# Split weights kept in device memory: a hybrid GLA/SSD block whose later token blocks load the parts

## The chip, the cores and the metric

The kernel runs on one core of a Trainium2 chip. The metric is device time in microseconds (us) of one execution. A core has five engines that work side by side and wait for each other by semaphores: TensorE (PE, matrix products; its weight loads are shown apart as PEld), VectorE (DVE), ScalarE (ACT), GpSimd (POOL) and SyncE (SP), which here only issues transfers. Transfers from device memory to on-chip memory run on 16 DMA engines.

## The reference

One layer over 2048 tokens of width 1024, in float32. Two mixers share one input projection: a gated linear attention with 4 heads and a state-space scan with 16 heads in two groups. A gated embedding and a last norm follow.

```
u = rmsnorm(h, norm_w)
q, k, v, g, gate_lr, z, xbc, dt_raw = split(u @ w_in)
gla_out = rmsnorm(gla_chunked(q, k, v, log_a)) * silu(g)
xs, bm, cm = split(silu(causal_conv(xbc)))
y = rmsnorm_per_group((ssd_chunked(xs, dt, a_neg, bm, cm) + xs * d_skip) * silu(z))
h = h + concat(gla_out, y) @ w_out
h = h + sigmoid(rmsnorm(h) @ w_pe_gate) * (p @ w_pe)
out = rmsnorm(h)
```

## The kernel before

**Blocks.** The 2048 tokens are cut into NB = 4 blocks of TB = 512, one after the other; the states of both mixers go from block to block. Each block runs through the same 70 pieces of weight, so every weight is read from device memory four times.

**Split products.** A float32 operand is held as two parts of a faster type, `hi` (the value rounded) and `lo` (the rest), and each product is made of three matmuls: hi by hi, hi by lo, lo by hi. In `dense_t` these are L203, L204, L205 (24 matmuls of 512 columns for one weight), in `dense_n` L222, L224, L226 (48 matmuls of 256 or 288 columns), in `out_proj` L794, L795, L796, in the embedding L938, L939, L940. The activations' parts are made once per block; the weights' parts are made anew in each block.

**How a weight comes in.** `plan` (L114) lists the 4 x 70 weights in the order of use. `take_w` (L177) hands out the next one and sees to it that one more is prepared behind it. `prep_w` (L157) allots a raw tile (tag `wraw`, 2 buffers), loads 512 or 576 KB into it from SP's queue (L164), and splits it in two halves: ACT casts the half to `whi` (L172), DVE subtracts to get `wlo` (L173). `whi` and `wlo` have 4 buffers each, so two weights can be held in parts:

```
s = raw[:, i * hn:(i + 1) * hn]
nc.scalar.copy(out=hi, in_=s)
tt(out=lo, in0=s, in1=hi.bitcast(F32), op=ALU.subtract)
```

**Side work.** Recurrences and norms are generators that `step()` (L184) moves on by one piece after each dense product. `ssd_steps` (L510) walks over 4 pieces of 128 tokens: it loads a decay tile `em` twice and `ec` (SP, L550 and L561), turns `em` into the decay mask with four DVE operations (L552), an exponential on ACT (L555) and a product (L556), and TensorE uses it in L579; `em` has 3 buffers. `ec` is used at L588, the state is updated at L587. `gla_steps` (L455) walks over the same pieces for one head: L451 to L453 and L488 on TensorE, L486 on DVE. `u_steps` (L321) loads the next block's input piece by piece (`xp`, SP, L327) and turns it into `u` on DVE (L328), ACT (L329) and POOL (L331). `final_steps` (L608) of a block runs in the next one: DVE writes the result into `ht` (L627) and POOL's queue sends it out in four stores (L629); then SP loads the next block's `ht`, 2 MB, at L851.

**Order.** The program is written in the order above; a scheduler with a time model of its own then sets each engine's order among what the dependences allow, and each engine and each queue runs its list strictly in order. So whatever waits at the head of SP's list holds back all transfers behind it. The results of dense products lie in 4 buffers (`psd`), those of the side work in 4 others (`pss`); TensorE waits when the next of them has not been emptied. The copy of the embedding product to `pp` (L941, ACT) is such an emptying.

Of the kernel before, what the change touches and what calls it, by code (L numbers as in the profile page):

```python
# [6 lines left out]
F32 = mybir.dt.float32  # L7
F32R = mybir.dt.float32r
# [3 lines left out]
ALU = mybir.AluOpType  # L12
# [23 lines left out]
def hybrid_kernel(ctx, tc, x_nat, x_t, p_t, w_t, w_n0, w_n, w_o, w_g, w_p, prm, gup, cst, out):  # L36
    nc = tc.nc
    mm = nc.tensor.matmul
    act = nc.scalar.activation
    tt = nc.vector.tensor_tensor  # L40
    stt = nc.vector.scalar_tensor_tensor
    NB = x_t.shape[0]
# [4 lines left out]
    wp = ctx.enter_context(tc.tile_pool(name="wp", bufs=2))  # L47
    sb = ctx.enter_context(tc.tile_pool(name="sb", bufs=2))
# [3 lines left out]
    dr = ctx.enter_context(tc.tile_pool(name="dr", bufs=2, space=DRAM))  # L52
# [45 lines left out]
    for h in range(GH):  # L98
        t = state.tile([P, 256], F32, name=f"gT{h}")
# [3 lines left out]
    for g in range(2):  # L103
        t = state.tile([P, 512], F32, name=f"sS{g}")
# [3 lines left out]
    for h in range(GH):  # L108
        t = sm.tile([P, NT + 1], F32, name="gD", tag=f"gD{h}", bufs=2)
# [3 lines left out]
    LAST_TAGS = {KT - 4: ("qm", "km", "qm", "km"), KT - 3: ("em", "em", "em", "amh")}  # L113
    plan = []  # L114
    for b in range(NB):
        def natural(src):
            plan.extend((src[i], 1152 if src is w_n0 else 1024, None) for i in range(2))

        def tseq(lst, tags=None):
            plan.extend((s, 1024, tags) for s in lst)  # L120

        def oseq(q):
            plan.extend((w_o[q, i], 1024, None) for i in range(4))

        natural(w_n0)
        if b == 0:
            natural(w_n[0])
        tseq([w_t[T_B], w_t[T_C]] + [w_t[T_XS + i] for i in range(2)])
        if b:
            natural(w_n[0])  # L130
        tseq([w_t[T_XS + i] for i in range(2, 4)])
        tseq([w_t[T_Q], w_t[T_K], w_t[T_Q + 1], w_t[T_K + 1]])
        tseq([w_t[T_Z + i] for i in range(4)])
        natural(w_n[1])
        natural(w_n[2])
        tseq([w_t[T_B + 1], w_t[T_C + 1]])
        oseq(2)
        tseq([w_t[T_XS + 4 + i] for i in range(2)])
        natural(w_n[3])
        tseq([w_t[T_XS + 4 + i] for i in range(2, 4)])  # L140
        natural(w_n[4])
        tseq([w_t[T_Q + 2], w_t[T_K + 2]])
        oseq(0)
        natural(w_n[5])
        natural(w_n[6])
        tseq([w_t[T_Q + 3], w_t[T_K + 3]])
        tseq([w_t[T_Z + 4 + i] for i in range(4)])
        oseq(1)
        oseq(3)
        for i in range(8):  # L150
            if i % 4 == 0:
                tseq([w_p[i // 4]])
            tseq([w_g[i]], LAST_TAGS.get(i) if b == NB - 1 else None)
    ready = []
    cursor = [0]

    def prep_w(raw=None):  # L157
        if cursor[0] == len(plan):
            return
        src, n, tags = plan[cursor[0]]  # L160
        cursor[0] += 1
        if raw is None:
            raw = wp.tile([P, n], F32, name="wraw", tag="wraw", bufs=SB["wraw"])
            nc.sync.dma_start(out=raw, in_=src)  # L164
        res = []
        hn = n // 2
        for i in range(2):
            pool, th, tl = (sb, tags[2 * i], tags[2 * i + 1]) if tags else (wp, "whi", "wlo")
            hi = pool.tile([P, hn], F32R, name="whi", tag=th, bufs=SB[th])
            lo = pool.tile([P, hn], F32R, name="wlo", tag=tl, bufs=SB[tl])  # L170
            s = raw[:, i * hn:(i + 1) * hn]
            nc.scalar.copy(out=hi, in_=s)  # L172
            tt(out=lo, in0=s, in1=hi.bitcast(F32), op=ALU.subtract)  # L173
            res.append((hi, lo))
        ready.append(res)
# [495 lines left out]
    for b in range(NB):  # L671
# [188 lines left out]
        v1, _ = dense_v(1)  # L860
# [18 lines left out]
        v3, _ = dense_v(3)  # L879
# [47 lines left out]
        for d, cs in jobs:  # L927
            n = cs.stop - cs.start
            if d % 4 == 0 and cs.start == 0:
                wpe = take_w()  # L930
                pp = sb.tile([P, 4, TB], F32, name="pp", tag="xs", bufs=SB["xs"])
                for j in range(4):
                    pps = psd.tile([P, TB], F32, name="psd")
                    for k in range(2):
                        sl = slice(j * P, (j + 1) * P)
                        hi, lo = wpe[k]
# [11 lines left out]
            th = sb.tile([P, n], F32, name="gth", tag="tmp", bufs=SB["tmp"])  # L948
# [101 lines left out]
```

## Time and profile before

| | before |
|---|---|
| median of 3 runs | 1922.84 us (1921.1 to 1924.56) |
| profiled execution, span | 1915.8 us |
| TensorE busy | 1848.5 us, 96% |
| TensorE's weight loads | 1577.9 us, 82% |
| VectorE busy | 1402.0 us, 73% |
| ScalarE busy | 929.5 us, 49% |
| GpSimd busy | 372.3 us, 19% |
| DMA | 206.56 MB, 108 GB/s over the span |

The span is the profiled execution's own time from its first to its last instruction; the runs are timed from outside, and their median is 7.0 us longer. Busy time is what an engine's instructions cover; matmuls overlap, so a busy TensorE can still be short of its best.

### The profile page before, as it was taken

The numbers are of one execution on the slowest core, as the hardware profiler recorded it, in microseconds if no ns is written. First come the engines' busy times: TensorE is split into PE (matmuls) and PEld (weight loads), VectorE is DVE, ScalarE is ACT, GpSimd is POOL, SyncE is SP. The second block draws the span as 40 slices with busy tenths as digits, with TensorE's granted clock in tenths as the row PEclk, the third lists the DMA queues.
The fourth block names the chain that finished last, engine by engine and source line by source line (L and its number), as shares of the span: only waits on it lengthen the run. The fifth ranks groups of instructions, "written<-read, shape, count | busy, mean of one in ns | idle before, by whom it ended". The sixth has DMA issues, their size and how long they took to land.

```text
span 1915.8 us, 27885 instructions
## 1 busy us (share of the span) xinstructions
PE 1848.5 (96%) x10418; PEld 1577.9 (82%) x10418; DVE 1402.0 (73%) x2689; ACT 929.5 (49%) x1692; POOL 372.3 (19%) x331
## 2 busy tenths in 40 slices
PE   8989999999999999999999999999999999999997
PEld 7868888877887888877788788897778788889886
DVE  8996686587788668558678766855877877684676
ACT  6545443465554553346555355334655445533563
POOL 3022031043112103004311210300430211030122
PEclk9999999999999999999999999999999999999998
DMA  4332242233443233223344323322334432232232
GB/s 138 121 110 88 79 158 73 88 110 122 170 125 100 82 107 125 77 78 110 124 177 121 101 77 115 117 89 77 123 113 165 135 97 78 92 104 82 68 119 77
DMA packets 80888, 206.56 MB, mean 108 GB/s; under 512 B 8048, under 2 KB 26736, under 8 KB 80368
## 3 DMA queue, kind: packets, MB, share of 16 engines
q1 hardware_dynamic: 78768, 198.21, 32.5%
q0 software_dynamic: 1984, 6.55, 0.9%
q8 instruction: 82, 1.34, 0.3%
q14 instruction: 54, 0.44, 0.1%
HBM read 196.09 MB, written 8.65 MB: 107 GB/s over the span
## 4 chain that ended last, share of the span: by engine, by line
PE 70%; DVE 18%; ACT 5%; issue 3%; DMA 3%; POOL 1%; SPq 0%; DVEq 0%; ACTq 0%; POOLq 0%
PE psd L204 10%; PE psd L203 10%; PE psd L205 10%; PE psd L224 5%; PE psd L226 5%; PE psd L222 5%; PE psd L796 5%; PE psd L795 5%; PE psd L794 5%; DVE em L552 3%; DVE wlo L173 3%; PE pss L488 1%; DMA xp<-x_t 1%; DMA em<-cd 1%; DVE em L556 1%
## 5 line engine op out<-in xcount | busy, mean ns | idle before, releaser
L173 DVE TENSOR_TENSOR wlo<-wraw,whi 128x512 fp32r<-128x512 f32 (+1 forms) x560 | 423.9, 761 | 218.7 <-ACT whi L172 217.3
L172 ACT CAST whi<-wraw 128x512 fp32r<-128x512 f32 (+1 forms) x560 | 343.9, 620 | 466.0 <-PE psd L204 238.2
L205 PE MATMUL psd<-u,wlo 128*128 128x512 f32 x896 | 352.7, 394 | 2.1 <-DVE wlo L173 2.1
L203 PE MATMUL psd<-u,whi 128*128 128x512 f32 x896 | 353.7, 395 | 0.0
L204 PE MATMUL psd<-u,whi 128*128 128x512 f32 x896 | 351.8, 393 | 0.9 <-POOL u L331 0.9
L222 PE MATMUL psd<-whi,u 128*128 128x256 f32 (+1 forms) x960 | 276.5, 288 | 0.0
L224 PE MATMUL psd<-wlo,u 128*128 128x256 f32 (+1 forms) x960 | 273.1, 284 | 2.1 <-DVE wlo L173 2.1
L226 PE MATMUL psd<-whi,u 128*128 128x256 f32 (+1 forms) x960 | 272.6, 284 | 0.0
L300 POOL TENSOR_TENSOR sq<-sq,sqt 128x512 f32<-128x512 f32 (+1 forms) x85 | 109.9, 1293 | 610.1 <-ACT sqt L297 610.1
L794 PE MATMUL psd<-mq,whi 128*128 128x512 f32 x512 | 205.4, 402 | 0.0
L796 PE MATMUL psd<-mq,wlo 128*128 128x512 f32 x512 | 202.1, 395 | 0.0
L795 PE MATMUL psd<-mq,whi 128*128 128x512 f32 x512 | 201.0, 393 | 0.0
L205 PEld LDWEIGHTS psd<-u,wlo 128*128 128x128 f32 x896 | 168.5, 188 | 39.4 <-DVE wlo L173 3.9
L204 PEld LDWEIGHTS psd<-u,whi 128*128 128x128 f32 x896 | 168.6, 188 | 34.1 <-POOL u L331 1.2
L203 PEld LDWEIGHTS psd<-u,whi 128*128 128x128 f32 x896 | 168.6, 188 | 33.5 <-ACT whi L172 0.6
L224 PEld LDWEIGHTS psd<-wlo,u 128*128 128x128 f32 x960 | 183.6, 191 | 5.3 <-DVE wlo L173 2.9
L222 PEld LDWEIGHTS psd<-whi,u 128*128 128x128 f32 x960 | 183.6, 191 | 2.4 <-ACT whi L172 1.0
L226 PEld LDWEIGHTS psd<-whi,u 128*128 128x128 f32 x960 | 183.6, 191 | 0.0
L797 DVE TENSOR_TENSOR ht<-ht,psd 128x512 f32<-128x512 f32 x128 | 86.9, 682 | 66.2 <-PE psd L796 65.9
L796 PEld LDWEIGHTS psd<-mq,wlo 128*128 128x128 f32 x512 | 96.3, 188 | 20.6 <-issue 0.7
L203 PE MATMUL psd<-mq,whi 128*128 128x512 f32 (+1 forms) x288 | 107.3, 373 | 5.8 <-ACT pp L941 5.8
L795 PEld LDWEIGHTS psd<-mq,whi 128*128 128x128 f32 x512 | 96.4, 188 | 20.0 <-DVE mq L505 1.1
(248 smaller groups left out, 3274.0 us busy)
## 6 DMA issues: line engine op xcount, KB each, us to landing
wraw<-w_t SPq DMA_DIRECT2D x112, 512.0 KB, 3.5
wraw<-w_o SPq DMA_DIRECT2D x64, 512.0 KB, 3.5
wraw<-w_n SPq DMA_DIRECT2D x56, 512.0 KB, 3.5
em<-cd SPq DMA_DIRECT2D x64, 256.0 KB, 3.9
wraw<-w_g SPq DMA_DIRECT2D x32, 512.0 KB, 3.6
ec<-ecd SPq DMA_DIRECT2D x64, 128.0 KB, 3.0
xn<-x_nat SPq DMA_DIRECT2D x24, 256.0 KB, 3.4
xp<-x_t SPq DMA_DIRECT2D x24, 256.0 KB, 3.8
```

The costliest lines, as they stand in the source:

```text
L172: nc.scalar.copy(out=hi, in_=s)
L173: tt(out=lo, in0=s, in1=hi.bitcast(F32), op=ALU.subtract)
L203: mm(out=ps, lhsT=hi[:, sl], rhs=rhi(k), start=(k == 0), stop=False)
L204: mm(out=ps, lhsT=hi[:, sl], rhs=rlo(k), start=False, stop=False)
L205: mm(out=ps, lhsT=lo[:, sl], rhs=rhi(k), start=False, stop=(k == KT - 1))
L222: mm(out=outs[t], lhsT=ug(0, k)[:, ts], rhs=hi[:, sl], start=first, stop=False, skip_group_check=True)
L224: mm(out=outs[t], lhsT=ug(0, k)[:, ts], rhs=lo[:, sl], start=False, stop=False, skip_group_check=True)
L226: mm(out=outs[t], lhsT=ug(1, k)[:, ts], rhs=hi[:, sl], start=False, stop=last, skip_group_check=True)
L300: self.eng.tensor_tensor(out=self.acc[:, cs], in0=self.acc[:, cs], in1=sq, op=ALU.add)
L794: mm(out=ps, lhsT=hi[:, sl], rhs=mq[:, 0, k, :], start=(k == 0), stop=False)
L795: mm(out=ps, lhsT=hi[:, sl], rhs=mq[:, 1, k, :], start=False, stop=False)
L796: mm(out=ps, lhsT=lo[:, sl], rhs=mq[:, 0, k, :], start=False, stop=(k == 3))
```

## The change

In block 0 (`split_w`) a weight is loaded and split as before, but both parts of a half go into one tile `whl` ([128, 2, n]; 4 buffers, the same bytes as `whi` and `wlo` had), and when the next weight is prepared, `save_w` writes these tiles to device memory from SP's queue: two stores of 512 KB (576 KB for `w_n0`) for each weight. In blocks 1 to 3 (`load_w`) nothing is split: the two halves of parts are loaded, 512 KB each, by two transfers on SP's queue. For two weights of three they go into `whl`, for the third into the buffers of `wraw`, so three weights can be held, and `take_w` prepares two ahead instead of one. The last block's weights with tags of their own come in four transfers of 256 KB. The tile `praw` (L912) moves from the buffers of `wraw` to that of `sg`. Line numbers behind the new functions are greater by 37: L550 is L587, L588 is L625, L627 is L664, L797 is L834, L851 is L888.

```diff
-SB = {"tmp": 4, "wraw": 2, "whi": 4, "wlo": 4, ...
+SB = {"tmp": 4, "wraw": 2, "whl": 4, ...
...
+    def save_w():
+        while unsaved:
+            dst, t = unsaved.pop(0)
+            nc.sync.dma_start(out=dst, in_=t.bitcast(F32))
+
+    def split_w(src, key, n, raw):
+        if raw is None:
+            raw = wp.tile([P, n], F32, name="wraw", tag="wraw", bufs=SB["wraw"])
+            nc.sync.dma_start(out=raw, in_=src)
+        save_w()
+        hn = n // 2
+        kept[key] = dr.tile([2, P, 2, hn], F32, name="wk_" + "_".join(map(str, key)),
+                            tag="wk_" + "_".join(map(str, key)), bufs=1)
+        res = []
+        for i in range(2):
+            t = wp.tile([P, 2, hn], F32R, name="whl", tag="whl", bufs=SB["whl"])
+            s = raw[:, i * hn:(i + 1) * hn]
+            nc.scalar.copy(out=t[:, 0, :], in_=s)
+            tt(out=t[:, 1, :], in0=s, in1=t[:, 0, :].bitcast(F32), op=ALU.subtract)
+            unsaved.append((kept[key][i], t))
+            res.append((t[:, 0, :], t[:, 1, :]))
+        return res
+
+    def load_w(key, n, tags, at):
+        save_w()
+        hn = n // 2
+        res = []
+        for i in range(2):
+            if tags:
...
+                continue
+            tg = "wraw" if at % 3 == 2 else "whl"
+            t = wp.tile([P, 2, hn], F32R, name="wkl", tag=tg, bufs=SB[tg])
+            nc.sync.dma_start(out=t.bitcast(F32), in_=kept[key][i])
+            res.append((t[:, 0, :], t[:, 1, :]))
+        return res
...
+        ready.append(split_w(src, key, n, raw) if pb_ == 0 else load_w(key, n, tags, at))
 
     def take_w():
-        while len(ready) < 2 and cursor[0] < len(plan):
+        while cursor[0] < len(plan) and len(ready) < (2 if plan[cursor[0]][3] == 0 else 3):
             prep_w()
         return ready.pop(0)
...
-        praw = wp.tile([P, 2 * TB], F32, name="praw", tag="wraw", bufs=SB["wraw"])
+        praw = sb.tile([P, 2 * TB], F32, name="praw", tag="sg", bufs=SB["sg"])
```

The engines' lists change in these places. In a row stand the line, the operation, what it writes and reads (with buffer numbers) and the size.

**SP, block 0, first group of `ssd_steps`** (`wraw` is a raw weight, `wk` a place in device memory, `em` and `ec` the decay tiles). Before:

```order
L164 DMA wraw_1003<-w_t 128x1024
L550 DMA em_970<-cd_846 128x512
L550 DMA em_978<-cd_846 128x512
L561 DMA ec_986<-ecd_848 64x4x128 x2
L550 DMA em_1076<-cd_846 128x512
L164 DMA wraw_1115<-w_t 128x1024
L164 DMA wraw_1366<-w_t 128x1024
L550 DMA em_1084<-cd_846 128x512
```

Now:

```order
L171 DMA wraw_1014<-w_t 128x1024
L166 DMA wk_t_21_937<-whl_938 128x1024
L587 DMA em_981<-cd_855 128x512
L587 DMA em_989<-cd_855 128x512
L598 DMA ec_997<-ecd_857 64x4x128 x2
L166 DMA wk_t_21_937<-whl_941 128x1024
L587 DMA em_1088<-cd_855 128x512
L171 DMA wraw_1127<-w_t 128x1024
L587 DMA em_1096<-cd_855 128x512
L166 DMA wk_t_25_1018<-whl_1019 128x1024
L166 DMA wk_t_25_1018<-whl_1022 128x1024
```

Two stores per weight now stand among the loads of the decay tiles.

**SP and DVE, early in block 1** (`ht` is the block's input of 2 MB; `n_1` is the gate's weight of head 0, used after four other weights). SP before:

```order
L164 DMA wraw_4965<-w_t 128x1024
L164 DMA wraw_5013<-w_n 128x1024
L164 DMA wraw_5077<-w_n 128x1024
L851 DMA ht_5311<-x_t 128x4096
L164 DMA wraw_5135<-w_t 128x1024
```

SP now:

```order
L202 DMA wkl_4967<-wk_t_5_650 128x1024
L202 DMA wkl_5009<-wk_n_1_0_284 128x1024
L888 DMA ht_5319<-x_t 128x4096
L202 DMA wkl_5011<-wk_n_1_0_284 128x1024
L202 DMA wkl_5051<-wk_n_1_1_375 128x1024
L202 DMA wkl_5053<-wk_n_1_1_375 128x1024
```

DVE before, the last block's result:

```order
L627 SCALAR_TENSOR_TENSOR ht_84<-ht_84,pr_82,rbc_4751 128x512
L173 TENSOR_TENSOR wlo_4842<-wraw_4839,whi_4841 128x512
L173 TENSOR_TENSOR wlo_4846<-wraw_4839,whi_4845 128x512
L627 SCALAR_TENSOR_TENSOR ht_84<-ht_84,pr_82,rbc_4751 128x512 x2
L173 TENSOR_TENSOR wlo_4918<-wraw_4915,whi_4917 128x512
L627 SCALAR_TENSOR_TENSOR ht_84<-ht_84,pr_82,rbc_4751 128x512
L173 TENSOR_TENSOR wlo_4922<-wraw_4915,whi_4921 128x512
```

DVE now:

```order
L664 SCALAR_TENSOR_TENSOR ht_84<-ht_84,pr_82,rbc_4813 128x512
L846 TENSOR_SCALAR lrn_4750<-psd_4756 128x4x16
L848 SCALAR_TENSOR_TENSOR dtr_4877<-psd_4756,pr_82 128x16
L851 TENSOR_TENSOR v_4872<-psd_4756,v_4872 128x256
L664 SCALAR_TENSOR_TENSOR ht_84<-ht_84,pr_82,rbc_4813 128x512 x7
```

The 2 MB load now stands between the two halves of one weight, and the eight operations that it waits for (by way of the stores) stand together, ahead of the products of the next weights. The same rows come again in blocks 2 and 3.

**DVE, block 1, second group of `ssd_steps`**, where `ec` is multiplied (L588, now L625). Before:

```order
L466 TENSOR_TENSOR amh_7410<-am_7407,amh_7410 128x512
L173 TENSOR_TENSOR wlo_7427<-wraw_7420,whi_7426 128x512
L797 TENSOR_TENSOR ht_5311<-ht_5311,psd_7430 128x512
L797 TENSOR_TENSOR ht_5311<-ht_5311,psd_7444 128x512
L173 TENSOR_TENSOR wlo_7512<-wraw_7509,whi_7511 128x512
L588 TENSOR_TENSOR ec_7398<-ec_7398,pss_7458 128x512
```

Now:

```order
L503 TENSOR_TENSOR amh_7244<-am_7241,amh_7244 128x512
L834 TENSOR_TENSOR ht_5319<-ht_5319,psd_7258 128x512
L834 TENSOR_TENSOR ht_5319<-ht_5319,psd_7272 128x512
L625 TENSOR_TENSOR ec_7232<-ec_7232,pss_7286 128x512
```

The two subtractions ahead of the product are gone, and nothing has come in their place.

## Rows read from the trace of the kernel before

**Rows 1.** The page, parts 1 and 3: busy time by engine; DMA queue, packets, MB, share.

```profile
PE 1848.5 (96%) x10418; PEld 1577.9 (82%) x10418; DVE 1402.0 (73%) x2689; ACT 929.5 (49%) x1692; POOL 372.3 (19%) x331
...
q1 hardware_dynamic: 78768, 198.21, 32.5%
```

**Rows 2.** Waits of TensorE in blocks 1 to 3: us in total, times, longest.

```profile
PE pss L451 <- DVE gT L486: 11.6, 6, 2.0
PE psd L203 <- ACT pp L941: 4.1, 2, 2.4
PE pss L459 <- DVE ec L588: 3.0, 3, 1.0
PE pss L267 <- POOL sq L300: 2.6, 2, 1.3
PE pss L451 <- DVE ec L588: 2.2, 2, 2.0
...
PE psd L224 <- DVE wlo L173: 1.6, 3, 0.5
PE psd L205 <- DVE wlo L173: 1.6, 3, 0.5
...
PE pss L451 <- DVE sS L587: 1.1, 3, 0.4
...
PE psd L940 <- DVE wlo L173: 0.9, 2, 0.6
```

**Rows 3.** Groups by line: busy us, mean ns of one, idle before.

```profile
L173 DVE TENSOR_TENSOR wlo<-wraw,whi 128x512 fp32r<-128x512 f32 (+1 forms) x560 | 423.9, 761 | 218.7 <-ACT whi L172 217.3
```

**Rows 4.** Timeline of block 1 from 768 us, DVE and TensorE: start, duration.

```profile
768.49 1.53 DVE L173 TENSOR_TENSOR wlo<-wraw,whi 128x512 fp32r<-128x512 f32 x1
...
771.14 0.68 DVE L173 TENSOR_TENSOR wlo<-wraw,whi 128x512 fp32r<-128x512 f32 x1
...
772.56 0.36 PE L451 MATMUL pss<-v,amh 128*128 128x256 f32 x1 [2.03 <-DVE ec L588]
```

**Rows 5.** One line's durations (min/median/max ns), then the timeline from 1056 us.

```profile
L552 DVE TENSOR_SCALAR em<-em,cum x256: 264/279/1528, 88.4 to 1713.0; 128x128 f32<-128x128 f32 x128
...
1056.13 3.48 DVE L552 TENSOR_SCALAR em<-em,cum 128x128 f32<-128x128 f32 x4
...
1060.00 0.39 PE L451 MATMUL pss<-v,kn 128*128 128x256 f32 x1 [1.94 <-DVE gT L486]
```

**Rows 6.** Timeline of block 1's end, DVE and TensorE.

```profile
937.34 0.75 DVE L328 SCALAR_TENSOR_TENSOR xp<-xp,pr,urb 128x512 f32<-128x512 f32 x1 [0.56 <-DMA xp<-x_t]
...
939.42 0.50 PE L203 MATMUL psd<-mq,whi 128*128 128x512 f32 x1 [2.36 <-ACT pp L941]
```

**Rows 7.** Stretches: busy us by engine (instructions), TensorE's clock, DMA share, GB/s.

```profile
12.00:485.00 473.00, 456.81 (x2561) 388.00 (x2561) 359.38 (x670) 236.59 (x434) 100.07 (x80) 1.00 0.33 105
...
240.00:288.00 48.00, 46.90 (x310) 40.86 (x308) 38.65 (x73) 21.09 (x44) 14.51 (x16) 1.00 0.47 154
...
768.00:816.00 48.00, 45.97 (x314) 42.12 (x313) 26.38 (x53) 14.85 (x31) 1.60 (x2) 0.96 0.25 77
```

**Rows 8.** Issue to landing of the loads of `em`, and DVE's wait for them.

```profile
  DMA em<-cd: 5.5, 8
...
DMA to landing us min/median/max: 3.0/3.9/6.2
```

**Rows 9.** Timeline of block 1 from 506 us: SP, POOL's queue, TensorE; landing of `ht`.

```profile
512.65 0.53 POOL L629 DMA_DIRECT2D out_t<-ht  x1 [2.18 <-DVE ht L627]
...
516.80 0.33 SPq L851 DMA_DIRECT2D ht<-x_t  x1
...
DMA to landing us min/median/max: 7.8/7.8/7.8
...
521.98 0.28 PE L222 MATMUL psd<-whi,u 128*128 128x256 f32 x1
522.10 0.28 PE L224 MATMUL psd<-wlo,u 128*128 128x256 f32 x1
```

More of the change, by code (lines that the diff above doesn't have):

```diff
@@ L27 @@
 M_ID, M_TRI, M_ONE, M_N = 0, 128, 256, 384
-SB = {"tmp": 4, "wraw": 2, "whi": 4, "wlo": 4, "rb": 1, "urb": 1, "v": 1, "amh": 1, "bc": 2, "sg": 1, "qm": 2, "km": 2, "kn": 1, "st": 2,
+SB = {"tmp": 4, "wraw": 2, "whl": 4, "rb": 1, "urb": 1, "v": 1, "amh": 1, "bc": 2, "sg": 1, "qm": 2, "km": 2, "kn": 1, "st": 2,
       "bt": 1, "ctl": 1, "xs": 1, "cb": 1, "bn": 1, "xd": 2, "xh": 1, "ec": 1, "em": 3, "sq": 1, "lrT": 1}
@@ L116, in natural, with tseq @@
         def natural(src):
-            plan.extend((src[i], 1152 if src is w_n0 else 1024, None) for i in range(2))
-        def tseq(lst, tags=None):
-            plan.extend((s, 1024, tags) for s in lst)
+            if src == 0:
+                plan.extend((w_n0[i], ("n0", i), 1152, b, None) for i in range(2))
+            else:
+                plan.extend((w_n[src - 1, i], ("n", src, i), 1024, b, None) for i in range(2))
+        def tseq(*lst):
+            plan.extend((w_t[j], ("t", j), 1024, b, None) for j in lst)
         def oseq(q):
-            plan.extend((w_o[q, i], 1024, None) for i in range(4))
-        natural(w_n0)
+            plan.extend((w_o[q, i], ("o", q, i), 1024, b, None) for i in range(4))
+        natural(0)
         if b == 0:
-            natural(w_n[0])
-        tseq([w_t[T_B], w_t[T_C]] + [w_t[T_XS + i] for i in range(2)])
+            natural(1)
+        tseq(T_B, T_C, T_XS, T_XS + 1)
         if b:
[L130 to L136, printed above, removed]
-        oseq(2)
[L138 to L142, printed above, removed]
+            natural(1)
+        tseq(T_XS + 2, T_XS + 3)
+        tseq(T_Q, T_K, T_Q + 1, T_K + 1)
+        tseq(*(T_Z + i for i in range(4)))
+        natural(2)
+        natural(3)
+        tseq(T_B + 1, T_C + 1)
+        oseq(2)
+        tseq(T_XS + 4, T_XS + 5)
+        natural(4)
+        tseq(T_XS + 6, T_XS + 7)
+        natural(5)
+        tseq(T_Q + 2, T_K + 2)
         oseq(0)
[L144 to L147, printed above, removed]
+        natural(6)
+        natural(7)
+        tseq(T_Q + 3, T_K + 3)
+        tseq(*(T_Z + 4 + i for i in range(4)))
         oseq(1)
@@ L151, in hybrid_kernel @@
             if i % 4 == 0:
-                tseq([w_p[i // 4]])
-            tseq([w_g[i]], LAST_TAGS.get(i) if b == NB - 1 else None)
+                plan.append((w_p[i // 4], ("p", i // 4), 1024, b, None))
+            plan.append((w_g[i], ("g", i), 1024, b, LAST_TAGS.get(i) if b == NB - 1 else None))
     ready = []
     cursor = [0]
+    kept = {}
+    unsaved = []
+    def save_w():
[25 more added lines that the diff above has]
+            if tags:
+                pair = []
+                for j in range(2):
+                    tg = tags[2 * i + j]
+                    t = sb.tile([P, hn], F32R, name="wsp", tag=tg, bufs=SB[tg])
+                    nc.sync.dma_start(out=t.bitcast(F32), in_=kept[key][i, :, j, :])
+                    pair.append(t)
+                res.append(tuple(pair))
+                continue
[4 more added lines that the diff above has]
+        return res
     def prep_w(raw=None):
@@ L159, in prep_w @@
             return
-        src, n, tags = plan[cursor[0]]
+        src, key, n, pb_, tags = plan[cursor[0]]
+        at = cursor[0]
         cursor[0] += 1
[L162 to L175, printed above, removed]
+        ready.append(split_w(src, key, n, raw) if pb_ == 0 else load_w(key, n, tags, at))
     def take_w():
-        while len(ready) < 2 and cursor[0] < len(plan):
+        while cursor[0] < len(plan) and len(ready) < (2 if plan[cursor[0]][3] == 0 else 3):
             prep_w()
```

## The prediction

> **What bounds the kernel now.** I read the busy times first, then who TensorE waits for, then the timeline around the longest of these waits. TensorE is busy for 1848.5 of 1915.8 us; DVE, which splits the weights, for 1402.0 [rows 1]. So the kernel is bound by TensorE's matmuls, of which the change takes none away, and a lighter DVE is worth only what TensorE waits for it. All that TensorE is idle is 1915.8 - 1848.5 = 67.3 us, its start and end and block 0 among it: more than this can't be had, however much DVE work goes. The list of waits says which part hangs on the splits: in blocks 1 to 3 the waits that bear on this sum to 28.7 us, and only three of the rows (1.6, 1.6 and 0.9 us) name a split itself [rows 2]. The others name an operation that stood in DVE's or ACT's list behind something, and the timeline tells behind what [rows 4 to 6].
>
> **What goes.** 560 subtractions take 761 ns on average [rows 3]; 420 of them, with as many casts on ACT, belong to blocks 1 to 3, some 320 us of DVE time. They lie beside the matmuls, so I cost them by the waits, not by their length.
> 1. The three rows that name a split: 1.6 + 1.6 + 0.9 = **-4.1 us** [rows 2]. The split is gone; what TensorE waits for in its place is a load, which is ordered two weights ahead.
> 2. Waits for `ec` and `sS`, 3.0 + 2.2 + 1.1 = 6.3 us [rows 2]. In block 1 the product for which TensorE waited 2.03 us stood behind splits of 1.53 and 0.68 us [rows 4], and both are missing from DVE's new list there. But the run of DVE work began with the decay tiles, whose part of the delay stays. Bounds 2.2 (that one place) and 6.3; I take **-4.5 us**, nearer to the upper end since in DVE's lists the other places look alike.
> 3. Waits for `gT`, 11.6 us in six [rows 2]. Here DVE was held by four operations on `em`, 3.48 us where the median of one is 279 ns, 1.1 us for four [rows 5]. No split is in that stretch, so most stays. Bounds 0 and 6 x 0.68 = 4.1 (one split of [rows 4] less ahead of each); I take **-2 us**, as one split stands ahead in about half of the cases.
> 4. Waits for `pp` and for the sum of squares, 4.1 + 2.6 = 6.7 us [rows 2]. The copy to `pp` stands in ACT's list behind a cast that waits for `xp`, on whose load DVE was still waiting [rows 6]; the splits that held the SP queue and DVE's list there go, the load's flight stays. Bounds 0 and 6.7; I take **-3 us**, a little under half.
> 5. After the wait of item 2 TensorE ran at half clock (1.2 instead of 2.4 GHz) for a while: 0.96 granted over 48 us [rows 7], so 0.04 x 48 = 1.9 us lost. Bounds 0 and 1.9; if the wait goes, so may this: **-1 us**.
>
> **What comes.**
> 6. Block 0 moves three times the weight bytes. 70 weights are 36.8 MB; the parts are twice that, 73.7 MB, written in 473 us, 156 GB/s more. The queue's 198.21 MB took 32.5% of the span [rows 1], so the engines at full work move 198.21 / (0.325 x 1915.8 us) = 318 GB/s. Block 0 goes from 105 to 261, and its busiest stretch from 154 to 310 GB/s [rows 7], 97% of 318. The Trainium skill (DMA: Bandwidth & Descriptors, Specifications) gives about 358 GB/s as the memory limit of a core; by that figure the stretch would be at 87%, and this item could be near 0. What it costs is the lateness of small loads: `em` lands after 3.9 us as a rule and 6.2 at worst, but DVE waited visibly for it for only 5.5 us in all [rows 8]. Three later pieces in each of two groups, six rounds, each 6.2 - 3.9 = 2.3 us later: 13.8 us if nothing hides it, 0 if all is hidden. I take a third, **+4.6 us**: the tile has a spare buffer, and most landings were hidden so far. The stores themselves wait for a split that SP's next raw load waited for before as well; behind them in SP's list stand raw loads, ordered two weights ahead.
> 7. In blocks 1 to 3 each weight is two loads, 1 MB. That is 105 + 78 = some 183 GB/s, 58% of 318, and a load is issued when the weight three places before it is used up, two weights ahead of need: at 473 us for 70 weights [rows 7] some 13 us, against 3.9 us for a typical landing [rows 8]. So the steady state is covered. The cover is thin at one place: the 2 MB load of `ht` stands before the second half of a weight. It took 7.8 us and was issued at 516.80, after the last store at 512.65; TensorE uses that weight from 521.98 on [rows 9]. In DVE's new list the results are finished in one run, so stores and load should go some 4 us earlier, and the half would land at about 512.6 + 7.8 + 1.6 (512 KB at 318 GB/s) = 522.0, just in time. Bounds 0 and the 10.5 us of the second rival; I take **+1 us**.
> 8. `praw` in another buffer, the wider tile, the four loads of 256 KB at the very end: 0; no row of TensorE's waits names what they touch, and the buffers are free by then.
>
> The sum is -4.1 - 4.5 - 2 - 3 - 1 + 4.6 + 1 = **-9.0 us**: the span goes from 1915.8 to 1906.8, and the median, 7.0 above the profiled span, from 1922.84 to **1913.8 us**, 0.47% less. A measurement of this kernel tells about 0.2%, 3.8 us, from no change.
>
> **The rivals.**
> - *The waits stay.* TensorE's long waits hang on decay tiles and `gT`, not on splits; then only item 1 is gained, block 0 still pays: -4.1 + 4.6 + 1 = +1.5, **1924.3 us**. For it: the largest row names `gT`, with no split in the stretch [rows 2, 5]. Against it: the places of item 2, where the splits can be seen [rows 4].
> - *Slower: the `ht` load blocks half a weight* in each of blocks 1 to 3. If the stores are no earlier than before, `ht` goes at 516.80 and lands 7.8 later, the half behind it 1.6 after that, at 526.2; it is needed six matmuls (0.12 us apart) after 521.98, at 522.7 [rows 9]. Three waits of 3.5 us are 10.5, and three times the half clock of item 5 adds 5.7: +16.2 instead of +1, in all +6.2, **1929.0 us**. It decides if `ht` is issued later than about 513. For it: the list puts it there in all three blocks, and SP can't pass it. Against it: the results come together in DVE's list now. The Trainium skill (DMA: Bandwidth & Descriptors, Queues, rings and completion order) says that a DMA engine takes the descriptors of a ring in order, by which the half could not overtake; that the landing of `em` ranges from 3.0 to 6.2 us on the same queue agrees with it.
> - *Block 0 is saturated.* Item 6 costs its full 13.8: -14.6 + 13.8 + 1 = +0.2, **1923.0 us**; with the first rival's small gain +10.7, **1933.5 us**. For it: 97% in one stretch [rows 7]. Against it: 82% over the block, and `em` was rarely waited for [rows 8].
> - That the splits remain can be ruled out: they are missing from DVE's list.
>
> **How the numbers follow.** The forecast gets 0.58, the first rival 0.14, the second 0.16, the third 0.12, a third of it with the first. Faster by over 0.2% is the forecast: 0.58. Within 0.2% are the first rival and two thirds of the third: 0.22. Slower are the second and the rest of the third: 0.20. The forecast's own range takes the bounds of its items: at best -4.1 - 6.3 - 4.1 - 6.7 - 1.9 with nothing paid, -23.1; all at once is unlikely, and I stop at -20, 1903. At the upper end it meets 1919. The range that holds the time 8 times in 10 reaches on to the second rival: **1903 to 1931 us**.
>
> **What would show it.** Right: 140 subtractions and casts instead of 560; no row of waits for a split after block 0; the waits for `ec` under 3 us in all, those for `gT` still near 10; no half clock at the place of 768 us; SP's queue moving some 382 MB (198 + 184); the idle time of blocks 1 to 3 down by some 14 us and block 0 longer by some 5. Wrong: a new row in which TensorE waits for a load of parts (`wkl`), above all some 33 us into each of blocks 1 to 3; `em` landing after 6 us as a rule in block 0, with DVE waiting; or a block 0 longer by 10 us or more.

## The result: 1902.8 us, faster than forecast

The changed kernel takes **1902.84 us** (median of 4 runs, 1899.13 to 1906.1), the kernel before 1923.38 us beside it: a ratio of 0.9891, 95% interval 0.9872 to 0.991. That is 20.5 us less, where 9.0 were forecast, and just outside the range of 1903 to 1931. The runs below were timed on several chips, each beside the kernel before. To compare them, each ratio to the kernel before is multiplied by 1923.4 us: the change gives **-21.0 us**. The half widths of the intervals are 3 to 5 us, so a difference of two such runs is uncertain by 4 to 6 us.

The page of the changed kernel, parts 1, 3 and 6:

```profile
PE 1840.8 (97%) x10418; PEld 1579.5 (83%) x10418; DVE 1113.7 (59%) x2269; ACT 698.0 (37%) x1272; POOL 355.1 (19%) x331
...
q1 hardware_dynamic: 129744, 382.39, 62.4%
...
wkl<-wk_t SPq DMA_DIRECT2D x168, 512.0 KB, 4.0
...
em<-cd SPq DMA_DIRECT2D x64, 256.0 KB, 4.2
```

DVE is 288.3 us lighter than in [rows 1] and the queue moves the 382 MB that were forecast. TensorE, the engine that bounds the kernel, is busy 7.7 us less with the same 10418 matmuls, and idle 62.0 us in place of 67.3. The splits' row shows 140 in place of the 560 of [rows 3], all in block 0:

```profile
L181 DVE TENSOR_TENSOR whl<-wraw,whl x140: 676/688/1784, 6.6 to 487.5; 128x512 fp32r<-128x512 f32 x136, 128x576 fp32r<-128x576 f32 x4
```

The stretches, in the columns of [rows 7]: block 0, its busiest slice, blocks 1 to 3.

```profile
12.00:485.00 473.00, 449.99 (x2508) 381.83 (x2507) 352.97 (x659) 230.59 (x424) 95.60 (x77) 0.99 0.74 253
240.00:288.00 48.00, 47.51 (x304) 41.83 (x303) 36.20 (x69) 22.52 (x46) 11.03 (x12) 1.00 0.92 307
497.00:1892.00 1395.00, 1372.06 (x7833) 1182.30 (x7831) 743.41 (x1567) 454.31 (x826) 250.59 (x232) 1.00 0.60 188
```

For blocks 1 to 3 the kernel before has this row, which did not stand ahead of the prediction:

```profile
485.00:1904.00 1419.00, 1383.96 (x7834) 1183.38 (x7832) 1030.60 (x1984) 683.73 (x1243) 267.43 (x233) 0.99 0.34 108
```

In the first 473 us TensorE gets through 2508 matmuls in place of 2561: block 0 pays. Afterwards nearly the same 7833 matmuls take 1395 us in place of 1419. TensorE's idle time there falls from 35.0 to 22.9 us, so by 12.1; its *busy* time falls by another 11.9. Block 1 begins with the first product that uses its first weight. From the span's start to there, block 0 is 497.1 us long (485.6 before), and blocks 1 to 3 together are 1405.8 (1430.2): +11.5 and -24.4.

TensorE's waits in blocks 1 to 3 of the changed kernel, from 504 us on, in the columns of [rows 2]:

```profile
PE pss L488 <- DVE gT L523: 11.7, 6, 2.0
PE psd L259 <- DMA wkl<-wk_n: 3.5, 2, 2.1
PE pss L312 <- POOL sq L337: 1.8, 1, 1.8
PE pss L488 <- DVE ec L625: 1.3, 2, 0.7
PE pss L304 <- POOL sq L337: 1.3, 2, 0.9
...
PE pss L488 <- DVE sS L624: 0.7, 2, 0.4
```

The splits, `pp` and the longer of the two `ec` rows of [rows 2] are gone, `gT` is untouched, and a load of parts is new. All rows of this view sum to 34.6 us before and 22.8 after. In block 0 they sum to 15.8 us before and 22.7 after, and the largest are now these:

```profile
PE pss L616 <- DVE em L593: 4.0, 3, 2.3
PE psd L261 <- DVE whl L181: 2.8, 2, 2.1
PE pss L304 <- POOL sq L337: 2.8, 1, 2.8
PE pss L488 <- DVE ec L625: 2.1, 2, 1.4
PE pss L488 <- ACT amh L502: 2.0, 1, 2.0
```

One plain error of the sum shows at once: a run is 1.8 us longer than its own span (1904.61 and 1902.8 here), not 7.0. The profiled execution of the kernel before was simply about 5 us quicker than the median run.

### The profile page after: what moved, and what is told of

It is laid out like the page before. It is cut to its first block, busy times and chain, and to the rows that moved or that the text cites. A ratio compares the mean times of both kernels' runs of the same rounds, so it can differ in the third digit from the quotient of the medians.

```text
span 1902.8 us, 27406 instructions
## 1 busy us (share of the span) xinstructions
PE 1840.8 (97%) x10418; PEld 1579.5 (83%) x10418; DVE 1113.7 (59%) x2269; ACT 698.0 (37%) x1272; POOL 355.1 (19%) x331
## 4 chain that ended last, share of the span: by engine, by line
PE 77%; DVE 11%; DMA 6%; ACT 3%; issue 2%; POOL 0%; SPq 0%; DVEq 0%; ACTq 0%; POOLq 0%
PE psd L240 12%; PE psd L242 12%; PE psd L241 12%; PE psd L259 6%; PE psd L261 6%; PE psd L263 6%; PE psd L833 5%; PE psd L831 4%; PE psd L832 4%; DVE em L589 2%; DMA em<-cd 2%; PE pss L525 1%; PE pss L616 1%; PE pss L488 1%; DMA xp<-x_t 1%
## 5 line engine op out<-in xcount | busy, mean ns | idle before, releaser
L240 PE MATMUL psd<-u,wkl 128*128 128x512 f32 x672 | 266.1, 396 | 0.0
L242 PE MATMUL psd<-u,wkl 128*128 128x512 f32 x672 | 264.8, 394 | 0.0
L241 PE MATMUL psd<-u,wkl 128*128 128x512 f32 x672 | 262.9, 391 | 0.0
L259 PE MATMUL psd<-wkl,u 128*128 128x256 f32 (+1 forms) x768 | 222.9, 290 | 3.5 <-DMA wkl<-wk_n 3.5
L261 PE MATMUL psd<-wkl,u 128*128 128x256 f32 (+1 forms) x768 | 219.5, 286 | 0.0
L263 PE MATMUL psd<-wkl,u 128*128 128x256 f32 (+1 forms) x768 | 219.5, 286 | 0.0
L831 PE MATMUL psd<-mq,wkl 128*128 128x512 f32 x384 | 154.9, 405 | 0.0
L391 DVE SCALAR_TENSOR_TENSOR acc<-psd,hcw,acc 128x511 f32<-128x511 f32 x144 | 107.0, 743 | 80.7 <-ACT acc L388 79.0
L259 PEld LDWEIGHTS psd<-wkl,u 128*128 128x128 f32 x768 | 147.9, 193 | 6.0 <-DMA wkl<-wk_n 3.9
L833 PE MATMUL psd<-mq,wkl 128*128 128x512 f32 x384 | 150.3, 393 | 0.0
L832 PE MATMUL psd<-mq,wkl 128*128 128x512 f32 x384 | 149.9, 392 | 0.0
L261 PEld LDWEIGHTS psd<-wkl,u 128*128 128x128 f32 x768 | 147.9, 193 | 2.0 <-issue 1.4
L242 PEld LDWEIGHTS psd<-u,wkl 128*128 128x128 f32 x672 | 126.3, 188 | 26.5 <-issue 0.5
L263 PEld LDWEIGHTS psd<-wkl,u 128*128 128x128 f32 x768 | 147.9, 193 | 0.0
L240 PEld LDWEIGHTS psd<-u,wkl 128*128 128x128 f32 x672 | 126.5, 188 | 24.9 <-issue 0.4
L241 PEld LDWEIGHTS psd<-u,wkl 128*128 128x128 f32 x672 | 126.4, 188 | 24.5
L181 DVE TENSOR_TENSOR whl<-wraw,whl 128x512 fp32r<-128x512 f32 (+1 forms) x140 | 109.0, 783 | 51.5 <-ACT whl L180 51.2
L834 DVE TENSOR_TENSOR ht<-ht,psd 128x512 f32<-128x512 f32 x128 | 87.0, 683 | 87.8 <-PE psd L833 87.7
L180 ACT CAST whl<-wraw 128x512 fp32r<-128x512 f32 (+1 forms) x140 | 85.1, 618 | 106.0 <-PE psd L242 27.8
L589 DVE TENSOR_SCALAR em<-em,cum 128x128 f32<-128x128 f32 x256 | 97.0, 444 | 13.0 <-DMA em<-cd 12.9
L242 PE MATMUL psd<-u,whl 128*128 128x512 f32 x224 | 88.4, 394 | 0.5 <-DVE whl L181 0.5
```

The costliest lines, as they stand in the source:

```text
L181: tt(out=t[:, 1, :], in0=s, in1=t[:, 0, :].bitcast(F32), op=ALU.subtract)
L240: mm(out=ps, lhsT=hi[:, sl], rhs=rhi(k), start=(k == 0), stop=False)
L241: mm(out=ps, lhsT=hi[:, sl], rhs=rlo(k), start=False, stop=False)
L242: mm(out=ps, lhsT=lo[:, sl], rhs=rhi(k), start=False, stop=(k == KT - 1))
L259: mm(out=outs[t], lhsT=ug(0, k)[:, ts], rhs=hi[:, sl], start=first, stop=False, skip_group_check=True)
L261: mm(out=outs[t], lhsT=ug(0, k)[:, ts], rhs=lo[:, sl], start=False, stop=False, skip_group_check=True)
```

## The experiments

**Which part pays, which part gains.** Theory 1: what the splits cost is the room they take in DVE's and ACT's in-order lists (relief). Theory 2: the weights are simply there earlier. Theory A: block 0's price is the stores. The first run keeps only the stores, the second only the loads.

```
-        ready.append(split_w(...) if pb_ == 0 else load_w(...))
+        ready.append(split_w(src, key, n, raw, pb_, tags))
...
```

(`split_w` stores its parts only where `pb_` is 0.)

> Block 0 as in the changed kernel (every weight split and both parts stored); blocks 1 to 3 load the raw weight and split it as the kernel before did, two weights ahead. The stored parts are never read. Theory A (the stores alone cost block 0 its 11.5 us, and the gain of the later blocks hangs on what is missing here): before plus 11.5, about 1935 us, 1930 to 1938. Rival B (block 0 is longer for its new order and its wider tile and a part of it is made good later): 1923 to 1929 us, and block 1 begins less than 8 us later than in the kernel before.

1930.56 us, ratio 1.0035 (1.0021 to 1.0048): **+6.7 us**, at the lower edge of theory A's range. Blocks 1 to 3 of its profile last 1429.8 us, as before, so none of block 0's loss is made good later.

```
-            unsaved.append((kept[key][i], t))
+            if cursor[0] <= 6:
+                unsaved.append((kept[key][i], t))
...
```

> Blocks 1 to 3 load 1 MB of ready parts per weight as in the changed kernel, but only the first six weights of block 0 are stored, and each later weight is one of these six (so the products of blocks 1 to 3 use other weights; the bytes loaded, and all work on the engines, are those of the changed kernel). Theory A (block 0's 11.5 us come from the 67 MB of stores): 1902.8 - 11 = about 1892 us, 1889 to 1895. Rival B (they come from the new order and the wider tile): 1900 to 1904 us. If the two are half and half, 1897.

1896.7 us, 0.9856 (0.9839 to 0.9873): -27.7, so the stores cost 27.7 - 21.0 = **6.7 us**, the same from the other side. It is the number for half and half: less than the 11.5 of the two profiles, and block 0 is still 490.9 us long here. Without stores, or with six, block 0 is 485.6 to 491.2 us long in seven profiled executions, so single profiles scatter by 5 us there.

```
             nc.sync.dma_start(out=t.bitcast(F32), in_=kept[key][i])
+            nc.scalar.copy(out=t[:, 0, :], in_=t[:, 0, :].bitcast(F32))
+            tt(out=t[:, 1, :], in0=lo, in1=lo, op=ALU.max)
```

> The changed kernel, but in blocks 1 to 3 every loaded half goes through one copy on ACT and one operation of two inputs on DVE of the split's size again, both of which leave the values as they are (high part copied onto itself, low part's maximum with itself). Loads, stores and the depth of three stay. Theory 1 (relief: the gain of 24.5 us in blocks 1 to 3 comes from the splits that are gone from DVE's and ACT's lists): most of it is lost, 1918 to 1930 us. Theory 2 (the weights are there earlier, since they are loaded three ahead and need no preparation): most of it stays, 1903 to 1909 us.

1944.74 us, 1.0113 (1.0093 to 1.0133): +21.7, worse than either theory said. It points to theory 1, but is no clean undoing: DVE now waits for each landing in its list (86.6 us for `wk_t` alone), where the raw loads of the kernel before came earlier.

```
-        while ... len(ready) < (2 if plan[cursor[0]][3] == 0 else 3):
+        while ... len(ready) < 2:
```

> The changed kernel with weights taken two ahead in blocks 1 to 3 in place of three. Theory 1 (relief of DVE and ACT): the load of a weight still comes some 6.6 us or more ahead of its use, 1902 to 1907 us, with a few more waits for loads. Theory 2 (early weights): waits for loads of parts in all three blocks, 1910 us or more.

1906.48 us, 0.99 (0.9882 to 0.9918): -19.2, inside theory 1's range. The third weight ahead is worth 1.8 us, under what this comparison can tell. Theory 2 falls.

**What the splits cost.** Now splits that nobody waits for. The first run of this pair has none in blocks 1 to 3 and loads 512 KB per weight; the second adds splits into a spare buffer.

```
...
+        t = wp.tile([P, n], F32R, name="wkl", tag="whl", bufs=SB["whl"])
+        nc.sync.dma_start(out=t.bitcast(F32), in_=kept[key])
+        return [(t[:, i * hn:(i + 1) * hn],) * 2 for i in range(2)]
...
```

> As the run with six stores, but blocks 1 to 3 load one weight's high parts only (512 KB in place of 1 MB) and use them for both parts (so the low parts are left out of the products of blocks 1 to 3). No splits, no stores, the weight traffic of the kernel before. Theory A (the doubled loads of blocks 1 to 3 cost next to nothing): 1894 to 1898 us, against 1896.7 with the doubled loads. Rival B (the doubled loads make other loads late): under 1892 us.

```
+            nc.scalar.copy(out=dum[:, 0, :], in_=s)
+            tt(out=dum[:, 1, :], in0=s, in1=dum[:, 0, :].bitcast(F32), op=ALU.subtract)
```

> As the run with half loads, but in blocks 1 to 3 each loaded half is also split on ACT and DVE into a buffer that nothing reads; TensorE takes the loaded tile and waits for no split. The work on ACT and DVE and the weight traffic are those of the kernel before. Theory 1 (relief: what the splits cost is the time they take in the in-order lists of ACT and DVE, ahead of other work): most of the gain goes, 1912 to 1922 us. Theory 2 (what they cost is TensorE's wait for the split weight itself): 1894 to 1900 us.

Half loads: 1888.5 us, 0.9826 (0.9811 to 0.9842), **-33.5**, rival B's number; so the doubled loads cost 33.5 - 27.7 = 5.8 us. Idle splits: 1922.26 us, 0.9995 (0.998 to 1.0011), **-1.0**. TensorE waits for no split in blocks 1 to 3 of this kernel, and yet it is as slow as the kernel before. So the 32.5 us between these two runs, nearly all of the splits' price, come from the room that they take beside other work, not from TensorE's wait for them. Blocks 1 to 3 of the half loads, then of the idle splits:

```profile
486.00:1875.00 1389.00, 1370.18 (x7831) 1180.78 (x7830) 748.53 (x1567) 454.64 (x826) 251.16 (x232) 1.00 0.33 110
```

```profile
488.00:1910.00 1422.00, 1384.46 (x7826) 1186.55 (x7824) 1046.55 (x1984) 679.45 (x1241) 267.00 (x233) 0.99 0.33 107
```

The second has every engine's busy time within 2% of the kernel before. Its waits there, of which the half loads have only `gT` (11.7) above 2 us:

```profile
PE pss L484 <- DVE gT L519: 11.4, 7, 2.0
PE pss L300 <- POOL sq L333: 6.7, 6, 2.1
PE pss L492 <- DVE ec L621: 3.4, 3, 1.9
PE pss L612 <- DVE em L589: 3.4, 2, 1.7
PE psd L971 <- DVE gth L982: 2.8, 2, 2.2
```

None names a split. Its own group in DVE's lines shows why it holds so much:

```profile
L197 DVE TENSOR_TENSOR dum<-wkl,dum 128x512 fp32r<-128x512 f32 (+1 forms) x420 | 315.0, 775 | 171.8 <-ACT dum L196 171.1
```

A subtraction holds DVE's list 775 ns while it runs and, on average, 171.8 / 420 = 0.41 us before that, nearly all of it waiting for its cast. One rival stays open in part: the scheduler orders each kernel anew. Of DVE's 2129 other operations, 1896 stand in the same order with and without the idle splits, and POOL's list is the same; no run holds the rest in place.

**Which list.** Only the casts (the second of the two added lines left out), then only the subtractions:

```
-            nc.scalar.copy(out=dum[:, 0, :], in_=s)
-            tt(out=dum[:, 1, :], in0=s, in1=dum[:, 0, :].bitcast(F32), op=ALU.subtract)
+            tt(out=dum[:, 1, :], in0=s, in1=t[:, (1 - i) * hn:(2 - i) * hn].bitcast(F32), op=ALU.subtract)
```

> As the run with idle splits (1922.3 us; without any splits 1888.5), but only the casts on ACT are done in blocks 1 to 3, into a buffer that nothing reads; no subtractions on DVE (and the low parts left out of the products, as there). If the relief is DVE's list: 1889 to 1895 us. If it is ACT's list: 1912 us or more. If both count: in between.

> As the run with idle splits, but only the subtractions on DVE are done in blocks 1 to 3 (of the loaded halves, into a buffer that nothing reads); no casts on ACT. If the relief is DVE's list: 1912 to 1922 us. If it is ACT's list, or the subtraction's wait for the cast: under 1900 us.

Casts alone: 1890.25 us, 0.9822 (0.9799 to 0.9845), -34.2: 420 casts of 618 ns cost nothing. Subtractions alone: 1912.85 us, 0.9948 (0.9928 to 0.9967), -10.0: **23.5 us**. The other 9.0 come only when both are there. This does not part the subtractions' work from their waiting: without casts they stand in DVE's list waiting for the loads, 148.4 us in all, nearly as long as for casts.

```profile
L196 DVE TENSOR_TENSOR dum<-wkl 128x512 fp32r<-128x512 f32 (+1 forms) x420 | 325.5, 802 | 148.4 <-DMA wkl<-wk_n 75.9 <-DMA wkl<-wk_t 72.0
```

In the run with casts alone ACT was idle 291.0 us ahead of its casts, waiting for loads, and nobody minded:

```profile
L196 ACT CAST dum<-wkl 128x512 fp32r<-128x512 f32 (+1 forms) x420 | 243.6, 618 | 291.0 <-DMA wkl<-wk_n 157.1 <-DMA wkl<-wk_t 133.0
```

**Why block 0 pays.** Bytes, or SP's list? First an eighth of the bytes with every store in its place:

```
...
+            else:
+                unsaved.append((thin[i], t[:, :, 0:64]))
...
```

> As the run with six stores (1896.7 us; later weights taken from these six, so the products of blocks 1 to 3 use other weights), but every other half of block 0 is stored too, only its first 64 of 512 columns: as many stores in SP's list and as many waits for splits there as in the changed kernel, with an eighth of the bytes. Theory A (bytes on the DMA engines make block 0 longer): 1896 to 1899 us, block 0 at most 4 us longer than without stores (485.6 to 490.9). Rival B (a store that waits for its split holds SP's list and the small loads behind it): 1901 to 1904 us, block 0 at 495 us or more.

1897.85 us, 0.9865 (0.9839 to 0.9891), -26.0: thin stores cost 1.7 us, whole ones 6.7. Yet SP was held at the thin stores, waiting for splits, nearly as long as at the whole ones of the changed kernel:

```profile
SPq L166 <- DVE whl L185: 283.5, 117, 10.1
```

```profile
SPq L166 <- DVE whl L181: 308.9, 124, 10.4
```

So it points to bytes, as theory A has it, though the two intervals reach 3 and 5 us to each side and the profile's block 0 (492.5 us) is 2.5 us short of rival B's 495, less than the scatter. In the DMA engines' time the thin stores are more than an eighth of the whole ones: between 12 and 485 us the engines were busy for 0.48 of it, with six stores only 0.37, with whole ones 0.74.

Then the whole stores from ACT's list in place of SP's:

```
-            nc.sync.dma_start(out=dst, in_=t.bitcast(F32))
+            nc.scalar.dma_start(out=dst, in_=t.bitcast(F32))
```

> The changed kernel with the stores issued from ACT's list in place of SP's. Theory A (the stores' 6.1 us in block 0 come from their bytes on the shared DMA engines): 1901 to 1905 us, no change. Rival B (they come from SP's one list, in which a store that waits for a split, or the bytes ahead in the same queue, hold the small loads behind it): 1896 to 1899 us. Rival C (ACT's list is held at each store until DVE has split): over 1907 us.

1929.41 us, 1.0039 (1.0025 to 1.0053), +7.5: rival C, ACT's list. A store there waits for DVE's subtraction with ACT's own work behind it (86 of the 140 stores are issued within 0.1 us of their subtraction's end), and block 0 grows to 519.9 us. Whether the queue itself matters stays open.

Then from SP's again, but with the last two stores always left for the next weight:

```
-        save_w()
+        save_w(2)
```

> The changed kernel, but the stores of a weight are issued one half weight to one weight later in SP's list, so that they wait less for a split. Rival B (SP's list holds the small loads behind a store): SP waits clearly less than 309 us for splits at its stores, and 1896 to 1901 us. Theory A (bytes): 1901 to 1905 us.

1901.04 us, 0.988 (0.9857 to 0.9902), -23.1. SP's waits for subtractions at its stores fall from 308.9 to 147.9 us (another 148.4 now stand at its raw loads), and the gain of 2.1 us is under what can be told. As the waits have mostly moved to the raw loads of the same list, this run does not decide between the two. What the bytes do is seen in `em`'s landing in block 0 of the changed kernel, 3.3 to 5.6 with a median of 4.9 us, where half loads have 3.7 and the kernel before 4.0:

```profile
em<-cd SPq DMA_DIRECT2D x16, 256.0 KB, 4.9
xn<-x_nat SPq DMA_DIRECT2D x8, 256.0 KB, 5.3
```

**The load of `ht`.** Eight pieces of 256 KB, one behind each of the next eight weights, in place of one load of 2 MB:

```
-            nc.sync.dma_start(out=ht, in_=x_t[b])
+            ht_left.extend((ht[:, k, :], x_t[b, :, k, :]) for k in range(KT))
...
```

(`load_w` then issues one piece behind each weight.)

> The changed kernel, but the 2 MB load of ht in blocks 1 to 3 goes as eight loads of 256 KB, one behind each of the next eight weights. If the two waits for the second half of a weight (2.28 and 1.57 us in blocks 2 and 3) and the half clock after the first come from the 2 MB ahead of it: these waits go, 1896 to 1901 us. Rival (loads of 1 MB per weight are late by themselves): the waits stay under another weight, 1901 to 1905 us.

1899.67 us, 0.9858 (0.9831 to 0.9884): -27.3. No wait for a load of parts is left in blocks 1 to 3, which last 1398.8 us in place of 1405.8. The place in the changed kernel, SP's queue and TensorE in block 2:

```profile
989.88 0.33 SPq L888 DMA_DIRECT2D ht<-x_t  x1
990.32 1.42 SPq L202 DMA_DIRECT2D wkl<-wk_n  x3
...
996.48 0.28 PE L261 MATMUL psd<-wkl,u 128*128 128x256 f32 x1
996.60 0.28 PE L263 MATMUL psd<-wkl,u 128*128 128x256 f32 x1
998.99 0.39 PE L259 MATMUL psd<-wkl,u 128*128 128x256 f32 x1 [2.12 <-DMA wkl<-wk_n]
```

`ht` landed at 997.67 us, 7.79 after its issue; the three halves issued behind it landed at 998.95, 1000.25 and 1001.53, one every 1.3 us. TensorE waited for the first. The Trainium skill (DMA: Bandwidth & Descriptors, Queues, rings and completion order) has the descriptors of a ring taken in order; these four landings, in the order of issue, agree; the spread of `em`'s landings, which the prediction names, could not show it. This row shows another thing: matmuls that start every 0.12 us are shown 0.28 long, so a listed wait of 2.12 us cost 2.27 from start to start. About 0.15 us of each wait stands in TensorE's *busy* time.

**Both together** (the edits of the late stores and of the pieces), **then beside the changed kernel on one chip.**

> The later stores and the eight pieces of ht together. If both help and add up: 1891 to 1898 us, faster than the changed kernel by 5 us or more. If only the pieces help: 1896 to 1901. If neither: 1901 to 1905 us.

> The changed kernel once more, beside the next one on the same chip: 1900 to 1906 us.

> The later stores and the eight pieces of ht once more, beside the changed kernel on the same chip. If the gain of 5.0 us between chips holds: 1895 to 1900 us and 3 to 7 us under the changed kernel. Rival: within 2 us of it.

1897.84 us, 0.986 (0.9835 to 0.9885), the first time; the second time 1899.66 us, 0.988 (0.9861 to 0.99), beside 1905.81 us, 0.9907 (0.9881 to 0.9932), for the changed kernel. By the ratios this version is 5.9 and 5.2 us ahead of the changed kernel; in each pair the intervals still overlap, and the waits that went are the better evidence. It is clearly ahead of the kernel before.

**The kernel before once more.**

> The kernel before once more, for a second profiled execution. If the profile on record was one of its faster executions (its span is 7.0 us under the median of the runs, of which only 1.8 us lie around the span), this one has a span of about 1921 us, and block 1 begins 3 to 6 us later than at 485.6 us. Rival: a span within 2 us of 1915.8, and something else lies around it.

A span of 1917.2 us and a time of 1919.0; block 1 begins at 487.9. By its number that is the rival, but nothing else lies around the span: this kernel's eight runs went from 1917.78 to 1927.43 us, with a median of 1922.5, each 1.8 us longer than its own span. So the profiled execution was again a quick one. Where a run of 1927 loses its time no profile shows.

**The same relief without the traffic?** If DVE's list is the price, the subtractions could move to POOL's, in the kernel before, for all halves and for each second one:

```
-            tt(out=lo, in0=s, in1=hi.bitcast(F32), op=ALU.subtract)
+            nc.gpsimd.tensor_tensor(out=lo, in0=s, in1=hi.bitcast(F32), op=ALU.subtract)
```

```
+            (nc.gpsimd.tensor_tensor if i else tt)(out=lo, in0=s, in1=hi.bitcast(F32), op=ALU.subtract)
```

> The kernel before, with every subtraction of a split on POOL in place of DVE; nothing is stored, nothing loaded twice, the reference is computed in full. A like subtraction takes POOL 1.31 us, so 560 of them some 735 us on an engine that was busy for about a fifth of the span. Theory 1 (the relief is DVE's list, 24 to 34 us in three blocks): 1885 to 1900 us, if POOL's list carries nothing that TensorE waits for. Rival (the splits then hold the sums of squares and the scaled inputs behind them in POOL's list): 1905 to 1925 us, with new waits for POOL.

> The kernel before, with the subtraction of every weight's second half on POOL, that of the first half on DVE as before. Theory 1: about half of the relief, 1900 to 1912 us, and under the run with all of them on POOL only if POOL's list holds something up there. Rival (the list is held by the wait for the cast, not by the length of the subtractions): 1918 us or more.

2021.87 us, 1.0517 (1.0493 to 1.054), and 1964.13 us, 1.0221 (1.0199 to 1.0243): +99.4 and +42.5. The first is far beyond both ranges, the second within its rival's open one. Groups of the run with all of them on POOL:

```profile
L173 POOL TENSOR_TENSOR wlo<-wraw,whi 128x512 fp32r<-128x512 f32 (+1 forms) x560 | 767.1, 1382 | 682.6 <-ACT whi L172 600.5 <-PE psd L226 44.8 <-PE psd L205 17.6
```

and TensorE's waits over its span:

```profile
PE pss L267 <- POOL sq L300: 17.0, 4, 5.3
PE pss L579 <- DVE em L556: 16.6, 9, 3.4
PE pss L468 <- DVE sS L587: 11.2, 8, 2.1
PE pss L453 <- DVE amh L466: 8.2, 4, 2.0
```

A subtraction takes 1.38 us there, and POOL stands 600.5 us at them waiting for casts, with the sums of squares and the states behind. So POOL's list is a worse place for them. How much of the loss comes from their length, from their waits and from DVE's operations that grow longer beside them (last section) these two runs do not part.

## Why the prediction was wrong, step by step

The mechanism was right in the main, on both sides: splits hold up other work in the lists, and block 0 pays for the stores. Only ACT's share of it did not show, since the casts alone cost nothing. The gain was sized at less than half.

| term | forecast | measured |
|---|---|---|
| TensorE no longer waits for splits (item 1) | -4.1 us | -1.0 (idle splits against the kernel before) |
| splits gone from the lists of blocks 1 to 3 (items 2 to 5) | -10.5 | -32.5 (half loads against idle splits) |
| stores in block 0 (item 6) | +4.6 | +6.7 (from both sides) |
| doubled loads with `ht` (item 7) | +1 | +5.8; the pieces of `ht` give back 6.3 |
| sum | -9.0 | -21.0 |

**The step that failed** is "They lie beside the matmuls, so I cost them by the waits, not by their length". Of the listed waits a fraction was taken, and they were taken for all there was: the upper bounds of items 1 to 5 add up to 23.1 us, and the runs give 33.5. The costs were sized too low as well, 5.6 us in place of 12.5, which hid over a third of the error in the gain. So it is luck that the time lies only 0.2 us outside the range: with 23.1 in place of the 20 at which it stopped, the range would have held it, and the step would have been as wrong.

- Item 1 (-4.1): the rows that name a split did go, but the idle splits show that taking away this wait alone gives 1.0 us, with an interval from 3.8 less to 2.1 more. In their place TensorE waits longer for other results: the listed waits are 36.8 us there, 34.6 before.
- Item 2 (-4.5): `ec` and `sS` at the same rows went from 6.3 to 2.0 us, -4.3. Right.
- Item 3 (-2): `gT` 11.6 to 11.7, nothing. Its signpost, "still near 10", was the better reading: no split stood in [rows 5].
- Item 4 (-3): `pp` 4.1 to none, the sum of squares 2.6 to 1.3, so -5.4; "a little under half" was too timid. That the cast in ACT's list did it is not shown: with casts alone no wait for `pp` is listed, with subtractions alone 1.2 us.
- Item 5 (-1): by the trace's clock record TensorE is granted half clock for 17.1 us in blocks 1 to 3 before the end, in the changed kernel for 10.2; with idle splits for 27.3, with half loads for 6.8. Half of that time is lost at most. I had priced one place only; by this estimate it is -3.4 here, and -10 from idle splits to half loads.
- "All that TensorE is idle is 67.3 us" was taken for the bound. It was not exceeded, but it was the wrong measure: half of the steady gain came out of the *busy* row: half clock, and the 0.15 us of each wait that the modelled ends hide. Of the 24.4 us between the two profiles the listed waits carry 11.8 and the clock 3.4; 16 waits fewer, at 0.15, another 2.4. For the last 7 I have no row.
- Item 6: the size was a little low. At 307 GB/s in the busiest slice `em` came later, as forecast, but `xn` and `ec` with it (5.3 and 5.0 us in place of 3.3 and 3.0). The path through `em` is not shown to be the whole of it: DVE waited 3.9 us for `em` in block 0, with thin stores 4.4. In the profile the 11.5 us are 6.9 more of listed waits and at most 5.1 for half clock (10.2 us of it in block 0, none before). And 318 GB/s was no ceiling: loads alone reached 403 GB/s between 995 and 1001 us of the changed kernel, which is also above the 358 that item 6 cites.
- Item 7 and the second rival: `ht` stood ahead of half a weight in all three blocks. In block 1 this half landed at 533.79 us and was needed at 534.18, so "just in time" was right there; in blocks 2 and 3 TensorE waited 2.1 and 1.4 us, not the rival's 3.5.
- The signs: nearly all those for "right" came, but so did two of those for "wrong", the row for `wkl` and a block 0 longer by more than 10 us in the profile. They could tell which things happen, not what each is worth.
- The median: 7.0 us above the span was not overhead but a quick profile. The changed kernel's, at 1904.61, was not; this alone is 5 us in comparing the two profiles.

**Carry over.** An instruction in a full in-order list can cost more than the rows that name it: here the rows that name a split gave 4.1 us, and the splits of three blocks cost 33.5. What it holds the list for ([rows 3]: 423.9 us of work, 218.7 of waiting) shows where to look, not the price. A two-sided test gives the price: do the suspected work where nobody waits for it, and leave it out, and take the difference. And a large load goes in pieces, behind what is needed next.

## Not expected of the hardware

TensorE's results (`psd`, `pss`) lie in the on-chip memory PSUM, the other tiles in SBUF. Many of DVE's operations with both inputs in SBUF grew long beside a busy POOL; those shown with one input in PSUM did not. The kernel before, then the one with all subtractions on POOL:

```profile
L906 DVE SCALAR_TENSOR_TENSOR mq<-ht,pr,mq 128x512 fp32r<-128x512 f32 x32 | 29.1, 939 | 1.9 <-ACT mq L905 1.9
...
L797 DVE TENSOR_TENSOR ht<-ht,psd 128x512 f32<-128x512 f32 x128 | 86.9, 682 | 66.2 <-PE psd L796 65.9
```

```profile
L906 DVE SCALAR_TENSOR_TENSOR mq<-ht,pr,mq 128x512 fp32r<-128x512 f32 x32 | 44.0, 1403 | 26.4 <-ACT mq L905 21.3 <-issue 5.1
...
L797 DVE TENSOR_TENSOR ht<-ht,psd 128x512 f32<-128x512 f32 x128 | 86.3, 680 | 89.1 <-PE psd L796 89.1
```

`mq` goes from 939 to 1403 ns, `ht` with `psd` stays at 682 and 680. Within the second run, of the 16 operations of L466 (both inputs in SBUF) the 12 that lie beside an operation of POOL took 1395 ns on average, the other four 680. Not all such operations grew: `xs<-xs,ec` (L592) takes 678 and 681. The Trainium skill (SBUF — State Buffer, SBUF: two separate sides) says that a DVE operation with two SBUF inputs and a GpSimd operation that reads SBUF lock a shared pair of ports against each other for their whole length; the trace agrees for those that grew. By that rule the change frees POOL too, and the same POOL work in blocks 1 to 3 takes 267.00 us with idle splits, 282.06 with subtractions alone and 251.16 without either. TensorE's listed waits for POOL there are 8.5, 8.3 and 2.6 us. So a part of the splits' price may come by way of POOL and not by DVE's list; no run parts the two.
